# Relative-bias rows of a decoder layer: one row store and one scratch-to-scratch copy in place of four spreads from a four-partition tile

## The chip, the core and the metric

The kernel runs on one core of one Trainium2 chip. The metric is the device time of one execution in microseconds (us). Everything is float32; the large matrix products are made from (high, low) pairs of parts, three matmuls each.

## The reference

One decoder layer on x (1, 512, 2048) with a memory mem (1, 256, 2048):

1. mix: one projection w_in feeds retention (8 heads) and sliding-window attention (16 query heads, 4 key-value heads, window 128) with a sink per head and a relative-position bias; the outputs go through w_o; x <- LN(alpha x + mix).
2. cross-attention with 4 heads of 512 into the 256 memory tokens; x <- LN(alpha x + xa).
3. gated feed-forward (5632 wide) with a causal convolution of width 3 on the gate; x <- LN(alpha x + ff).

What the change touches is the bias of the sliding window:

```
bias   = rel_bias[t5_bucket(max(dist, 0))]        # rel_bias (32 buckets, 16 heads), dist = i + 128 - j
logits = where(valid, q k^T * 64**-0.5 + bias, -inf)
m      = max(max(logits), sink);  p = exp(logits - m)
p      = p / (sum(p) + exp(sink - m))
```

For a head the bias depends on the distance alone, so a row of 255 values per head holds all of it. The 128 x 128 table that the kernel needs has, in partition p, that row from element 127 - p on.

## The kernel before

The layer runs in stages on one core: memory(), swa(), retention(), then the output projection, cross-attention and the feed-forward. Weights come as 1 MB chunks (chunk(), L86, on the SP queue, three raw buffers); ACT makes the high part whi (L73), VectorE the low part wlo (L74), and TensorE runs three matmuls per tile (mm3, L96 to L98).

memory() is the stage around the change. For each of the four cross-attention heads h it makes the keys (4 chunks xa_k) and values (4 chunks xa_v); folds the keys with wq (4 chunks xa_q) into blocks ao, stored to scratch a_sc (L225, SP); then multiplies the values by wo (4 chunks xa_o). This last product is four blocks cb of 24 matmuls of 512 columns each, into PSUM banks of tags B, A, B, A (two banks a tag). A block ends with two copies by VectorE from PSUM to a tile oo (L230), which has two buffers, and two stores o_sc<-oo of 256 KB (L232, SP).

The bias rows are made at the start by swa_tables (L237 to L250): three small loads on ACT's queue, one matmul (L246), and a copy by VectorE to br, a tile of 16 partitions (heads) x 256 (L248). br stays in SBUF. In each head of memory(), after the a_sc stores, swa_spread(h) (L252 to L256) writes four rows of br, each 128 times, to a scratch tensor br_sc of 128 x 4 x 256 (512 KB). The written access pattern is head, copy, element: 4 x 128 x 256. In swa() four tables tb (128 x 4 x 128) are loaded from those tensors on ACT's queue (L286), each partition one element earlier than the one before; VectorE adds them to the logits (L328).

Each engine and each queue works in order. The order of instructions on an engine is chosen by a scheduler that runs the program against a model of its time and may move an instruction ahead of those written before it once its inputs are ready. `keep_in_program_order` (in swa_spread) pins an instruction behind what is written before it on the same engine. Dependencies through scratch tensors are kept by semaphores.

Of the kernel before, what the change touches and what calls it, by code (L numbers as in the profile page):

```python
# [10 lines left out]
F32 = mybir.dt.float32  # L11
# [6 lines left out]
P = 128  # L18
# [6 lines left out]
SH = 16  # L25
# [11 lines left out]
class Layer:  # L37
# [23 lines left out]
        warm = self.cp.tile([P, 1], F32, name="warm")  # L61
        nc.scalar.copy(warm, self.mhalf[:, :1])

# [1 line left out]
    def n(self, s):  # L65
        self.uid += 1
        return f"{s}_{self.uid}"
# [13 lines left out]
        return [self.st.tile([P, 1024], F32R, name=self.n(t), tag=t, bufs=4) for t in ("whi", "wlo")]  # L81

    def chunk(self, src, halves=None):
        """One megabyte of weights, as two halves of (high, low) parts."""
        raw = self.st.tile([P, 2048], F32, name=self.n("raw"), tag="raw", bufs=3)
        self.nc.sync.dma_start(raw, src)  # L86
        res = []
        for h in range(2):
            hi, lo = (halves or self.halves)()
            self.split(hi, lo, raw[:, h * 1024:(h + 1) * 1024])  # L90
            res.append((hi, lo))
        return res
# [11 lines left out]
            self.mm3(ps[:, c], (hi[:, w], lo[:, w]), xs(k, c), k == 0, k == KT - 1)  # L104

    def ws(self, src, xs, n=S, tag="W"):
        """Feature-major product of one 128-column tile: [128 cols, n tokens]."""
        ps = self.bank(tag)
        self.ws_mm(ps, self.chunk(src), xs, slice(0, n))
        return ps  # L110

    def ws_pair(self, srcs, xs, tags=("W", "W")):
        """Two such tiles, the first half of the tokens ahead of the second."""
        pss = [self.bank(t) for t in tags]
        hvs = [self.chunk(s) for s in srcs]
        for c in (slice(0, 256), slice(256, 512)):
            for ps, hv in zip(pss, hvs):
                self.ws_mm(ps, hv, xs, c)
        return pss

    def as_block(self, chunks, xs, w, nt, done, kt=KT, tags="AABB"):
        """Token-major products of one block of w columns, nt token tiles."""
        if w == 512:
            acc = [self.bank(tags[t]) for t in range(nt)]
        else:
            b = [self.bank("A") for _ in range(nt // 2)]
            acc = [b[t // 2][:, t % 2 * 256:t % 2 * 256 + w] for t in range(nt)]
        kk = 1024 // w
        k0 = 0
        for src in chunks:  # L130
            for hi, lo in self.chunk(src):
                for t in range(nt):
                    for q in range(kk):
                        c = slice(q * w, (q + 1) * w)
                        self.mm3(acc[t], xs(k0 + q, slice(t * P, (t + 1) * P)), (hi[:, c], lo[:, c]),
                                 k0 + q == 0 and (w == 512 or t % 2 == 0),
                                 k0 + q == kt - 1 and (w == 512 or t % 2 == 1))
                    if k0 + kk == kt and w == 512:
                        done(t, acc[t])
                    elif k0 + kk == kt and t % 2:  # L140
                        done(t - 1, acc[t - 1])
                        done(t, acc[t])
                k0 += kk

    def as_last(self, hv, xs, w, nt, done, kt=KT):
        """As as_block, token tile by token tile."""
        kk = 1024 // w
        last = None
        for t in range(nt):
            acc = self.bank("AB"[t % 2])  # L150
            with self.tc.issue_after(last.ins) if t else nullcontext():
                for k in range(kt):
                    hi, lo = hv[k // kk]
                    c = slice((k % kk) * w, (k % kk + 1) * w)
                    last = self.mm3(acc[:, :w], xs(k, slice(t * P, (t + 1) * P)), (hi[:, c], lo[:, c]),
                                    k == 0, k == kt - 1)
            done(t, acc[:, :w])
# [4 lines left out]
        self.nc.sync.dma_start(r, src)  # L162
        self.split(self.ah[g], self.al[g], r)

# [1 line left out]
    def memory(self):  # L166
        nc, I = self.nc, self.I
        with ExitStack() as c:
# [38 lines left out]
            for h in range(XH):  # L207
                ks = proj("xa_k", h, pre if h == 0 else None)
                vs = proj("xa_v", h)
                if h == 1:  # L210
                    for g in range(4):
                        r = stage().rearrange("p (k s) -> p k s", k=4)
                        nc.sync.dma_start(r, I["xT"][:, 4 * g:4 * g + 4, :])
                        self.split(self.ah[g], self.al[g], r)
                for fq in range(4):
                    o = mp.tile([P, 4, ML], F32, name=self.n("ao"), tag="ao", bufs=2)
                    for hf, (hi, lo) in enumerate(self.chunk(I["xa_q"][4 * h + fq])):
                        ps = self.bank("T")
                        for i in range(2):
                            for k in range(4):  # L220
                                c = slice((4 * i + k) * P, (4 * i + k + 1) * P)
                                self.mm3(ps[:, i * ML:(i + 1) * ML], (hi[:, c], lo[:, c]), ks(k, slice(0, ML)),
                                         k == 0, k == 3)
                        nc.scalar.copy(o[:, 2 * hf:2 * hf + 2], ps.rearrange("p (i m) -> p i m", i=2))
                    nc.sync.dma_start(self.asc[h // 2][fq][:, :, h % 2 * ML:(h % 2 + 1) * ML], o)  # L225
                self.swa_spread(h)
                for cb in range(4):
                    def done(m, a):
                        o = mp.tile([P, S], F32, name=self.n("oo"), tag="oo", bufs=2)
                        nc.vector.tensor_copy(o, a)  # L230
                        k = 2 * h + m
                        nc.sync.dma_start(self.osc[cb][k // 4][:, k % 4], o)  # L232

                    self.as_block([I["xa_o"][4 * h + cb]], vs, 512, 2, done, 4, "AA" if cb % 2 else "BB")

# [1 line left out]
    def swa_tables(self, mp):  # L237
        nc, I, cp = self.nc, self.I, self.cp
        self.sink = cp.tile([P, SH], F32, name="sink")
        nc.scalar.dma_start(self.sink, I["swa_sinks"].broadcast_to([P, SH]))  # L240
        rb = mp.tile([32, SH], F32, name="rb")
        nc.scalar.dma_start(rb, I["rel_bias"])
        oh = mp.tile([32, 256], F32, name="oh")
        nc.scalar.dma_start(oh, I["c_onehot"])
        ps = self.bank("T")
        nc.tensor.matmul(ps[:SH, :256], rb, oh, start=True, stop=True)  # L246
        br = mp.tile([SH, 256], F32, name="br")
        nc.vector.tensor_copy(br, ps[:SH, :256])  # L248
        self.br = br
        self.brsc = []  # L250

    def swa_spread(self, g):  # L252
        t = self.dr.tile([P, 4, 256], F32, name=f"br_sc{g}")
        src = self.br[4 * g:4 * g + 4].unsqueeze(1).broadcast_to([4, P, 256])
        self.tc.keep_in_program_order(self.nc.sync.dma_start(t.rearrange("p h t -> h p t"), src))
        self.brsc.append(t)  # L256

    def swa(self):
        nc, I, sp = self.nc, self.I, self.sp
# [11 lines left out]
        for g2 in range(2):  # L271
# [9 lines left out]
            tbs = []  # L281
            for gg in range(2):
                tb = sp.tile([P, 4, P], F32, name=self.n("tb"), tag="tb", bufs=2)
                src = self.brsc[2 * g2 + gg]
                ap = bass.AP(tensor=src.tensor, offset=src.offset + 127, ap=[[4 * 256 - 1, P], [256, 4], [1, P]])
                nc.scalar.dma_start(tb, ap)  # L286
                tbs.append(tb)
            qs = {}
# [16 lines left out]
                        self.swa_out(g2, *p, vs)  # L305

    def swa_logits(self, g2, unit, qs, ks, tbs):
        """Probabilities of two heads in one block: column c stands for the one
        token of the window (of this block up to the diagonal, of the previous
        one above it) that lies at c."""  # L310
        nc, sp = self.nc, self.sp
        gg, b, m2 = unit
        lg = sp.tile([P, 2, P], F32, name=self.n("lg"), tag="lg", bufs=3)
# [132 lines left out]
        nc.scalar.activation(o, pt, AF.Copy, scale=gn[:, h:h + 1])  # L446
        return o

# [1 line left out]
    def affine(self, y, pool, gbc, bbc):  # L450
        nc = self.nc
        for q in range(4):
# [7 lines left out]
                nc.gpsimd.tensor_tensor(y[t][:, c], y[t][:, c], B, op=ALU.add)  # L460

    def post(self, y, blocks, xs, kt, lng, own=None):
        """y = norm(alpha * y + x @ w), token-major and in place; y * g + b feature-major."""
        nc, lp = self.nc, self.lp
        bs = [lp.tile([P, 4, 6], F32, name=self.n("lbs"), tag=f"lbs{t}") for t in range(NT)]

# [10 lines left out]
        w = 512  # L477
# [28 lines left out]

        self.as_last(hv, xs, w, NT, fin, kt)

# [1 line left out]
    def scores(self):  # L510
        nc, xp = self.nc, self.lp
        ph = [xp.tile([P, 4, S], F32R, name=f"ph{i}") for i in range(2)]
# [24 lines left out]
                          lambda t, a: soft(hp, t, a))  # L537
        return lambda k, c: (ph[k // 4][:, k % 4, c], pl[k // 4][:, k % 4, c])

# [1 line left out]
    def ffn(self, y):  # L541
        nc, I, fp = self.nc, self.I, self.fp
        cw = self.fp.tile([P, NFF, 4], F32, name="cw")
# [97 lines left out]
                nc.vector.scalar_tensor_tensor(v, v, rs, B[:, c], op0=ALU.mult, op1=ALU.add)  # L641
            nc.sync.dma_start(self.out[0, t * P:(t + 1) * P, c], v)

# [1 line left out]
    def run(self):  # L645
        nc, I = self.nc, self.I
        self.memory()
# [159 lines left out]
```

## Time and profile before

| | us |
|---|---|
| median of 3 runs (2902.71 to 2902.89) | 2902.73 |
| span of the profiled execution, first to last instruction | 2899.5 |
| TensorE busy (matmul) | 2796.2 |
| VectorE busy | 1298.5 |
| ACT (ScalarE) busy | 862.5 |
| POOL busy | 262.8 |

The profile gives the span of one execution; what it leaves out against the median of the runs is 3.2 us around it. PE is TensorE's matmuls and PEld its weight loads, DVE is VectorE, ACT ScalarE, POOL GpSimd; SPq and ACTq are the queues on which SP and ACT issue transfers. An instruction is named by its line, its operation and out<-in. PEclk is the clock granted to TensorE as a share of 2.4 GHz. Matmuls are pipelined, so the busy times of neighbours overlap. A wait is put down to the instruction that ended it.

### The profile page before, as it was taken

The numbers are of one execution on the slowest core, as the hardware profiler recorded it, in microseconds if no ns is written. First come the engines' busy times: TensorE is split into PE (matmuls) and PEld (weight loads), VectorE is DVE, ScalarE is ACT, GpSimd is POOL, SyncE is SP. The second block draws the span as 40 slices with busy tenths as digits, with TensorE's granted clock in tenths as the row PEclk, the third lists the DMA queues.
The fourth block names the chain that finished last, engine by engine and source line by source line (L and its number), as shares of the span: only waits on it lengthen the run. The fifth ranks groups of instructions, "written<-read, shape, count | busy, mean of one in ns | idle before, by whom it ended". The sixth has DMA issues, their size and how long they took to land.

```text
span 2899.5 us, 34839 instructions
## 1 busy us (share of the span) xinstructions
PE 2796.2 (96%) x14642; PEld 2399.3 (83%) x14642; DVE 1298.5 (45%) x1878; ACT 862.5 (30%) x1214; POOL 262.8 (9%) x244
## 2 busy tenths in 40 slices
PE   8789798999999999999999999999999999999997
PEld 8788787889989888978788888888888888888886
DVE  6334333666343443554654333433434343433356
ACT  5333332433222232232432223222222322232331
POOL 0000000223010100160260000000000000000003
PEclk9899898999999999999999999999999999999999
DMA  8656655222322253132232232232222323223241
GB/s 298 193 190 203 199 184 167 80 86 80 102 93 93 81 189 131 59 102 100 76 117 98 91 102 93 96 102 87 102 94 95 102 87 102 93 96 102 89 144 58
DMA packets 72061, 337.64 MB, mean 116 GB/s; under 512 B 7488, under 2 KB 24288, under 8 KB 35552
## 3 DMA queue, kind: packets, MB, share of 16 engines
q1 hardware_dynamic: 65232, 322.99, 32.7%
q10 hardware_dynamic: 6672, 12.43, 1.3%
q8 instruction: 115, 1.88, 0.3%
q14 instruction: 42, 0.34, 0.0%
HBM read 309.17 MB, written 26.21 MB: 116 GB/s over the span
## 4 chain that ended last, share of the span: by engine, by line
PE 61%; DVE 1%; POOL 1%; ACT 1%; issue 0%; DMA 0%; DVEq 0%; ACTq 0%; POOLq 0%
PE psT L96 6%; PE psT L97 6%; PE psT L98 6%; PE psW L96 5%; PE psW L97 5%; PE psW L98 5%; PE psA L96 5%; PE psA L97 5%; PE psA L98 5%; PE psB L96 4%; PE psB L98 4%; PE psB L97 4%; PE psT L495 0%; POOL y L459 0%; ACT xf L503 0%
## 5 line engine op out<-in xcount | busy, mean ns | idle before, releaser
L74 DVE TENSOR_TENSOR wlo<-raw,whi 128x1024 fp32r<-128x1024 f32 x532 | 671.0, 1264 | 1070.2 <-ACT whi L73 1068.4
L73 ACT CAST whi<-raw 128x1024 fp32r<-128x1024 f32 x532 | 557.9, 1051 | 1628.9 <-PE psW L97 597.4
L96 PE MATMUL psW<-ah,whi 128*128 128x512 f32 (+1 forms) x1136 | 443.7, 391 | 0.4 <-ACT ah L73 0.4
L98 PE MATMUL psW<-ah,wlo 128*128 128x512 f32 (+1 forms) x1136 | 442.7, 390 | 0.0
L97 PE MATMUL psW<-al,whi 128*128 128x512 f32 (+1 forms) x1136 | 441.6, 389 | 0.4 <-POOL al L74 0.4
L97 PE MATMUL psT<-al,whi 128*128 128x512 f32 (+1 forms) x720 | 276.8, 384 | 0.0
L98 PE MATMUL psT<-ah,wlo 128*128 128x512 f32 (+1 forms) x720 | 276.7, 384 | 0.0
L96 PE MATMUL psT<-ah,whi 128*128 128x512 f32 (+1 forms) x720 | 276.7, 384 | 0.0
L96 PE MATMUL psA<-whi,ah 128*128 128x256 f32 (+1 forms) x800 | 245.8, 308 | 6.2 <-ACT xp L523 3.0
L97 PEld LDWEIGHTS psW<-al,whi 128*128 128x128 f32 x1136 | 214.8, 189 | 44.0 <-POOL al L74 0.7
L96 PEld LDWEIGHTS psW<-ah,whi 128*128 128x128 f32 x1136 | 214.8, 189 | 43.7 <-ACT ah L73 0.9
L98 PEld LDWEIGHTS psW<-ah,wlo 128*128 128x128 f32 x1136 | 214.9, 189 | 42.4
L97 PE MATMUL psA<-wlo,ah 128*128 128x256 f32 (+1 forms) x800 | 245.1, 306 | 0.0
L98 PE MATMUL psA<-whi,al 128*128 128x256 f32 (+1 forms) x800 | 244.6, 306 | 0.0
L96 PEld LDWEIGHTS psA<-whi,ah 128*128 128x128 f32 x800 | 154.0, 192 | 14.3 <-ACT xp L523 3.5
L97 PEld LDWEIGHTS psA<-wlo,ah 128*128 128x128 f32 x800 | 153.9, 192 | 6.6
L98 PEld LDWEIGHTS psA<-whi,al 128*128 128x128 f32 x800 | 153.9, 192 | 6.5
L98 PEld LDWEIGHTS psT<-ah,wlo 128*128 128x128 f32 x720 | 135.3, 188 | 26.9
L97 PEld LDWEIGHTS psT<-al,whi 128*128 128x128 f32 x720 | 135.3, 188 | 26.9
L96 PEld LDWEIGHTS psT<-ah,whi 128*128 128x128 f32 x720 | 135.3, 188 | 26.8
L98 PE MATMUL psW<-mh,wlo 128*128 128x256 f32 x512 | 145.8, 285 | 1.5 <-DVE wlo L74 1.5
L96 PE MATMUL psW<-mh,whi 128*128 128x256 f32 x512 | 145.9, 285 | 0.9 <-ACT whi L73 0.9
(207 smaller groups left out, 4409.7 us busy)
## 6 DMA issues: line engine op xcount, KB each, us to landing
raw<-in_ffn_up SPq DMA_DIRECT2D x88, 1024.0 KB, 4.8
raw<-in_w_in SPq DMA_DIRECT2D x44, 1024.0 KB, 4.9
raw<-in_ffn_down SPq DMA_DIRECT2D x44, 1024.0 KB, 4.9
raw<-in_xa_v SPq DMA_DIRECT2D x16, 1024.0 KB, 7.0
raw<-in_xa_q SPq DMA_DIRECT2D x16, 1024.0 KB, 4.9
raw<-in_xa_o SPq DMA_DIRECT2D x16, 1024.0 KB, 5.9
raw<-in_w_o SPq DMA_DIRECT2D x16, 1024.0 KB, 4.8
raw<-in_xa_k SPq DMA_DIRECT2D x15, 1024.0 KB, 10.0
```

What stands on the lines that cost most here:

```text
L73: self.nc.scalar.copy(hi, src)
L74: (eng or self.nc.vector).tensor_tensor(lo, src, hi.bitcast(F32), op=ALU.subtract)
L96: mm(ps, a[0], b[0], start=start, stop=False)
L97: mm(ps, a[0], b[1], start=False, stop=False)
L98: return mm(ps, a[1], b[0], start=False, stop=stop)
```

## The change

The rows br are stored once to a scratch tensor brow (16 x 256, 16 KB), on ACT's queue, in swa_tables. swa_spread loses its argument and its pin, and is called in the first head alone: one transfer on ACT's queue reads the 16 KB of brow 128 times (a step of 0 outermost) and writes br_sc, now one tensor of 128 x 4096 (2 MB). The table loads take their rows from it: offset 4 (2 g2 + gg) 256 + 127, and a step of 16 x 256 - 1 = 4095 elements per partition instead of 1023. Comments are removed elsewhere.

```diff
-                self.swa_spread(h)
+                if h == 0:
+                    self.swa_spread()
...
         br = mp.tile([SH, 256], F32, name="br")
         nc.vector.tensor_copy(br, ps[:SH, :256])
-        self.br = br
-        self.brsc = []
-
-    def swa_spread(self, g):
-        t = self.dr.tile([P, 4, 256], F32, name=f"br_sc{g}")
-        src = self.br[4 * g:4 * g + 4].unsqueeze(1).broadcast_to([4, P, 256])
-        self.tc.keep_in_program_order(self.nc.sync.dma_start(t.rearrange("p h t -> h p t"), src))
-        self.brsc.append(t)
+        self.brow = self.dr.tile([SH, 256], F32, name="br_row")
+        nc.scalar.dma_start(self.brow, br)
+
+    def swa_spread(self):
+
+        self.brsc = self.dr.tile([P, SH * 256], F32, name="br_sc")
+        src = bass.AP(tensor=self.brow.tensor, offset=self.brow.offset, ap=[[0, P], [1, SH * 256]])
+        self.nc.scalar.dma_start(self.brsc, src)
...
                 tb = sp.tile([P, 4, P], F32, name=self.n("tb"), tag="tb", bufs=2)
-                src = self.brsc[2 * g2 + gg]
-                ap = bass.AP(tensor=src.tensor, offset=src.offset + 127, ap=[[4 * 256 - 1, P], [256, 4], [1, P]])
+                src = self.brsc
+                ap = bass.AP(tensor=src.tensor, offset=src.offset + 4 * (2 * g2 + gg) * 256 + 127,
+                             ap=[[SH * 256 - 1, P], [256, 4], [1, P]])
                 nc.scalar.dma_start(tb, ap)
```

## Rows read from the trace of the kernel before

**Rows 1.** The page's head and its totals: busy us (share of span) xinstructions.

```profile
span 2899.5 us, 34839 instructions
...
PE 2796.2 (96%) x14642; PEld 2399.3 (83%) x14642; DVE 1298.5 (45%) x1878; ACT 862.5 (30%) x1214; POOL 262.8 (9%) x244
```

**Rows 2.** Waits of TensorE, whole span: us in total, times, longest us.

```profile
PE psA L96 <- DVE oo L230: 66.5, 5, 15.9
```

**Rows 3.** Timeline of VectorE: start us, us, engine line, out<-in, [idle before <-releaser].

```profile
9.17 0.40 DVE L248 COPY br<-psT 16x256 f32<-16x256 f32 x1
...
113.92 0.69 DVE L230 COPY oo<-psA 128x512 f32<-128x512 f32 x1 [21.09 <-DMA o_sc<-oo]
```

**Rows 4.** Timeline of the SP queue in the first head.

```profile
86.00 0.57 SPq L255 DMA_DIRECT2D br_sc<-br  x1
86.69 6.40 SPq L86 DMA_DIRECT2D raw<-in_xa_k  x1
93.13 7.34 SPq L232 DMA_DIRECT2D o_sc<-oo  x2
```

**Rows 5.** Line L232 (o_sc stores): issue ns min/median/max, starts; then landing.

```profile
L232 SPq DMA_DIRECT2D o_sc<-oo x32: 319/320/3687, 93.1 to 457.5; - x32
...
DMA to landing us min/median/max: 2.9/7.5/21.1
```

**Rows 6.** Windows behind a spread: length, busy PE/PEld/DVE/ACT/POOL, PEclk, DMA share, GB/s.

```profile
90.00:92.00 2.00, 2.00 (x11) 1.58 (x10) 0.43 (x2) 1.05 (x1) 0.00 (x0) 1.00 0.22 24
...
104.00:106.00 2.00, 0.00 (x0) 0.00 (x0) 0.00 (x0) 0.00 (x0) 0.00 (x0) 0.50 0.70 127
```

**Rows 7.** Windows of the start, same columns.

```profile
15.00:20.00 5.00, 3.55 (x28) 3.14 (x27) 3.18 (x4) 2.93 (x4) 0.00 (x0) 1.00 1.01 428
20.00:25.00 5.00, 5.00 (x44) 5.00 (x44) 4.11 (x5) 3.30 (x4) 0.00 (x0) 1.00 1.01 421
```

**Rows 8.** Timeline of TensorE: the first and the last of the five waits.

```profile
114.75 0.76 PE L96 MATMUL psA<-whi,kvh 128*128 128x512 f32 x1 [15.87 <-DVE oo L230]
...
454.50 0.36 PE L96 MATMUL psA<-whi,ah 128*128 128x256 f32 x1 [2.87 <-DVE oo L230]
```

**Rows 9.** Windows around the four waits, and of stretches without one, same columns.

```profile
93.12:98.72 5.60, 5.60 (x25) 4.30 (x23) 0.00 (x0) 1.05 (x1) 0.00 (x0) 1.00 0.71 200
...
114.75:123.11 8.36, 8.36 (x25) 6.61 (x26) 4.54 (x5) 1.53 (x2) 0.00 (x0) 0.65 0.82 261
...
224.64:232.70 8.06, 8.06 (x25) 6.36 (x26) 4.54 (x5) 1.52 (x2) 0.00 (x0) 0.68 0.83 258
...
334.23:342.12 7.89, 7.89 (x25) 6.23 (x26) 4.54 (x5) 1.53 (x2) 0.00 (x0) 0.69 0.84 265
...
443.71:454.50 10.79, 7.93 (x24) 6.02 (x25) 6.03 (x8) 2.59 (x3) 0.00 (x0) 0.79 0.81 276
...
454.50:458.57 4.07, 4.07 (x21) 4.07 (x22) 2.82 (x3) 0.00 (x0) 0.00 (x0) 0.58 0.64 183
...
20.00:85.00 65.00, 65.00 (x535) 64.40 (x535) 39.71 (x37) 36.82 (x43) 0.00 (x0) 1.00 0.77 286
```

**Rows 10.** DMA issues: queue, xcount, KB each, median us from issue to landing.

```profile
raw<-in_ffn_up SPq DMA_DIRECT2D x88, 1024.0 KB, 4.8
...
a_sc<-ao SPq DMA_DIRECT2D x16, 512.0 KB, 3.5
...
raw<-in_ln_g ACTq DMA_DIRECT2D x1, 1024.0 KB, 4.7
...
gn<-in_gnT ACTq DMA_DIRECT2D x1, 4.0 KB, 5.0
```

**Rows 11.** Timeline of ACT's queue in the start.

```profile
7.11 0.35 ACTq L372 DMA_DIRECT2D gn<-in_gnT  x1
```

**Rows 12.** Tile tb: its readers and loads, duration ns, first and last start us.

```profile
L328 DVE CUSTOM_DVE_ANT_0 lg<-lg,tb,sink x64: 332/350/456, 520.8 to 699.5; 128x128 f32<-128x128 f32 x64
L286 ACTq DMA_DIRECT2D tb<-br_sc x4: 383/386/1156, 465.2 to 608.3; - x4
```

## The prediction

> **What bounds the kernel now.** I read the totals first: TensorE is busy for 2796.2 of the 2899.5 us span, and no other compute engine passes half [rows 1]. So the time is matmul time plus 103.3 us in which TensorE does nothing, and I asked next who leaves it idle. The waits of TensorE answer: 66.5 us, in only five waits, are the first matmul into a psA bank waiting for a copy to oo (L230) [rows 2]. VectorE's timeline carries it one step back: the copy at 113.92 had waited 21.09 us for an earlier store o_sc<-oo to land, since oo has two buffers [rows 3].
>
> The timeline of the SP queue shows what stands before those stores. In the first head the spread br_sc<-br (L255) is issued at 86.00; the raw load after it takes 6.40 us to issue, and the next two o_sc stores 7.34 together [rows 4], where the median store issue takes 0.32 [rows 5]. While the spread runs the DMA engines are mostly idle: 22% of sixteen busy (3.5 engines), 24 GB/s at 90 to 92 us [rows 6], against 421 to 428 GB/s at 101% when all work [rows 7]. At 24 GB/s the spread's 0.524 MB is 22 us of work. The reading: four engines serve the spread, and a load or store that uses all sixteen lands only when its share on those four is through.
>
> The first stall is 15.87 us long, before the matmul at 114.75; the smallest of the five waits, 2.87 us, stands at 454.50 [rows 8]. The other 66.5 - 2.87 = 63.6 us are four waits of nearly the same length, one per head of memory(), each some 13 us behind that head's spread.
>
> **Part 1, the four spreads go.** The waits: 63.6 us [rows 2, 8]. Then the clock. A block of 24 matmuls of 512 columns takes 5.60 us at full clock (93.12:98.72) [rows 9]. While TensorE idles the granted clock falls to 0.50, the 1.2 GHz level [rows 6], and the same 24 matmuls after the wait take 8.36, 8.06 and 7.89 us in heads 0 to 2: 2.76 + 2.46 + 2.29 = 7.51 us lost [rows 9]. In the last head, from 443.71 to 454.50, the block and the wait of 2.87 us take 10.79, so 10.79 - 5.60 = 5.19 [rows 8, 9]. Behind that wait 21 matmuls of 256 columns take 4.07 us at a mean clock of 0.58 [rows 9]; at the 5.00 us for 44 of the stretch 20:25 they would take 2.39, so 1.68 more [rows 7]. Together 63.6 + 7.51 + 5.19 + 1.68 = **78.0 us**. Between 20 and 85 us, with the same kinds of work and no spread, TensorE is never idle [rows 9], so work that is brought forward meets no other wait that the trace shows.
>
> What is late next where the stall was? The stores' own landing. An oo buffer is used again one block (5.60 us) later. With the copy's 0.69 us [rows 3] and the shortest landing, 2.9 us, its cycle is 3.6 and fits; with the median of 7.5 [rows 5] it is 8.2 and each block after the first would slip by 2.6 us, 7.8 for three, less the one block (5.6) by which a psA bank is freed ahead of its next use: 2.2 us a head, 9 for four. So a new stall of this kind costs 0 to 9 us. I take 0: the median includes the stores of the backlog, and a store twice as large (a_sc, 512 KB) lands in 3.5 us [rows 10].
>
> Four issues on SP disappear too. They cost nothing now, since the loads behind them run ahead into three raw buffers while TensorE works, and give nothing back; without that cover each is below one us.
>
> **Part 2, one row store and one copy are added on ACT's queue.** The 16 KB store brow<-br becomes ready when the copy to br ends, at 9.17 + 0.40 = 9.6 us [rows 3]; the spreading copy waits for it to land. The old spreads were pinned behind what precedes them on SP; the new pair is not. Unpinned ACT transfers float: the gn load (L372), written behind the whole of memory() and swa(), is issued at 7.11 us [rows 11]. So I expect the copy not at 86 us but near 9.6 + 0.4 (issue, as gn's) + 5.0 (landing, as gn's [rows 10]) = 15 us. Queued behind it on ACT are the casts whi, mh and ah of the first loads; VectorE's lo parts wait for those casts, and TensorE for both.
>
> The copy moves 128 x 16 KB = 2.10 MB. No row shows a scratch-to-scratch transfer. Its lower bound is 0, if it runs where the loads have lead. It can't gain: it adds bytes to engines that are already full. As DMA time at 421 GB/s it is 5.0 us [rows 7]. Reading one row many times is no penalty by itself: the ln3 gain, 1 MB fetched from one 8 KB row, lands in 4.7 us where an ordinary MB takes 4.8 [rows 10]. At the removed spreads' rate per engine (24 / 3.5 = 6.9 GB/s, sixteen of them 110) it is 19 us, all of which the start could lose. I take 5 for the whole start, nearest to that broadcast row: from 15 to 20 us the engines are full and TensorE is busy for 3.55 of 5.00 us only [rows 7], so 5.0 us of added traffic delay the raw loads by up to 5.0; some lead hides a part, and ACT standing at the wait for the row's landing adds as much again. Bounds: 0 to 19.
>
> The Trainium skill speaks against such a copy, in "DMA: Bandwidth & Descriptors", section "Bandwidth": it gives about 358 GB/s of HBM bandwidth per core. A copy that reads and writes HBM would carry 4.19 MB across it, 11.7 us by that figure as an estimate, and the sum would be 6.7 us worse. The trace differs for loads, with 421 to 428 GB/s; no row here has a copy within HBM.
>
> **Part 3, the table loads** tb (L286) step 4095 elements from partition to partition instead of 1023, with the same 512-byte runs. The first is issued at 465.2 and first used by VectorE at 520.8 [rows 12]; 55 us cover it, so 0. Uncovered, the slower of two landings would show once per pair of heads, a few us. Removed comments cost nothing.
>
> **Sum.** 78.0 - 5 = 73.0 us gained. The profiled span is 3.2 us below the median of the runs, 2902.73; I carry the difference over to the median: 2902.73 - 73.0 = **2829.7 us**.
>
> **Rivals.**
> *The copy is as slow per engine as the spreads and costs the start (chance 0.07).* For: the cause of that low rate is not in the rows. Against: the broadcast load at full rate. At 19 us: 2902.7 - 78.0 + 19 = 2843.7; with some us of lower clock 2847.
> *The stores themselves hold part of the wait (0.06).* For: the releaser named is a store, and the median landing is long [rows 3, 5]. Against: all five waits on oo stand in the backlog of a spread. If half of the gain stays away: 2902.7 - 39 + 5 = 2869.
> *Nothing moves (0.02).* If the loads and not the spreads held the queue, the same waits return; the 3.5 busy engines speak against it. About 2902.
> *Slower (0.04).* The copy again runs on about four engines. Then 2.10 MB at 24 GB/s take 87 us, in the start, where every 1 MB load needs its share of those four. If all 87 us reach TensorE, with some 3 of lower clock, it is 2902.7 - 78.0 + 90 = 2915. It decides from 78 us of lost start on. For: 3.5 busy engines is what the spreads showed [rows 6]. Against: the copy has 128 rows outermost on both sides where a spread had 4 heads, and it is on another queue than the loads, which are then beside it and not behind it.
> The Trainium skill, same page, section "Why a DMA increments its semaphore by 16 and not by 1", says that the number of engines is the largest up to 16 that divides the outermost size of both sides. That gives 4 for the spread, as the trace has it, and 16 for the copy; by it this rival falls away.
>
> **How the numbers follow.** The forecast has 0.81. Its own range is 2902.7 - 78.0 + 0 = 2825 to 2902.7 - 78.0 + 10 + 9 = 2844. Where the scheduler orders other work anew, some us may go either way, so the low end is 2821; the first rival moves the high end to 2847. What lies above is 0.12 in named rivals, with little below. A measurement of this kernel tells 0.2%, about 6 us, from no change: faster has 0.81 + 0.07 + 0.06 = 0.94, same 0.02, slower 0.04.
>
> **What would show it.** Right: TensorE's wait on oo falls from 66.5 to under 10 us, the raw load after the last a_sc store of a head issues in under 1 us, the clock stays at 1.00 through the four heads, and the last matmul of memory() comes some 70 us earlier. A copy at 10 to 20 us on ACT's queue, with casts waiting about 5 us more for raw loads or for the row, would confirm part 2. Wrong: an o_sc landing above 10 us, TensorE idle for over 10 us anywhere between 20 and 400 us, or a start that ends more than 20 us later.

## The result and the profile after

The changed kernel takes 2828.02 us (median of four runs, 2825.46 to 2831.51) against 2902.72 (four runs): a ratio of 0.9748, 95% interval 0.9734 to 0.9762. That is 74.7 us less; the two profiled spans differ by 2899.5 - 2826.7 = 72.8 us.

The totals of the changed kernel, for [rows 1], and two of its waits of TensorE, for [rows 2] (us in total, times, longest):

```profile
span 2826.7 us, 34831 instructions
...
PE 2787.4 (99%) x14642; PEld 2393.5 (85%) x14642; DVE 1298.1 (46%) x1878; ACT 862.7 (31%) x1214; POOL 263.1 (9%) x244
```

```profile
PE psW L96 <- ACT whi L73: 2.7, 2, 1.4
PE psA L96 <- DVE oo L231: 2.5, 1, 2.5
```

The five waits on oo, 66.5 us, have become one of 2.5. The timeline of the SP queue at the end of the first head shows why: with no spread behind the a_sc store, the raw load is issued in 0.42 us and two o_sc stores in 2.06, for 6.40 and 7.34 in [rows 4].

```profile
90.09 0.52 SPq L225 DMA_DIRECT2D a_sc<-ao  x1
90.87 0.42 SPq L86 DMA_DIRECT2D raw<-in_xa_k  x1
91.70 2.06 SPq L233 DMA_DIRECT2D o_sc<-oo  x2
```

That a_sc store, the last of the first head, stood at 85.43 in the kernel before:

```profile
85.43 0.53 SPq L225 DMA_DIRECT2D a_sc<-ao  x1
```

So the start has become 4.66 us longer. ACT's timeline there has the two new transfers, and the DMA issues say when they landed (KB, median us from issue to landing):

```profile
9.97 0.34 ACTq L251 DMA_DIRECT2D br_row<-br  x1
...
14.93 0.57 ACTq L257 DMA_DIRECT2D br_sc<-br_row  x1
```

```profile
br_sc<-br_row ACTq DMA_DIRECT2D x1, 2048.0 KB, 12.0
...
br_row<-br ACTq DMA_DIRECT2D x1, 16.0 KB, 4.9
```

Windows of the start (columns as in [rows 6]) answer to [rows 7]: TensorE is busy for 2.97 us instead of 3.55 between 15 and 20, and in this execution the granted clock then falls to a mean of 0.67, so that 32 matmuls fit where 44 did. The last row is the stretch behind the remaining wait, at the first product of swa(): 18 matmuls in 3.72 us at 0.54, as behind the same wait before ([rows 9]).

```profile
15.00:20.00 5.00, 2.97 (x22) 2.56 (x22) 2.74 (x4) 2.64 (x4) 0.00 (x0) 0.99 1.06 451
20.00:25.00 5.00, 5.00 (x32) 5.00 (x31) 3.42 (x4) 1.99 (x2) 0.00 (x0) 0.67 0.98 413
...
384.91:388.63 3.72, 3.72 (x18) 3.72 (x19) 1.58 (x2) 0.00 (x0) 0.00 (x0) 0.54 0.81 269
```

Longer windows show where the start lost its time. The first pair is the kernel before, the second the changed kernel, the third another profile of the changed kernel (the run j_after_again below), in which the a_sc store is at 90.69:

```profile
10.00:30.00 20.00, 17.55 (x134) 16.73 (x134) 14.70 (x17) 13.71 (x15) 0.00 (x0) 1.00 1.00 404
30.00:40.00 10.00, 10.00 (x86) 10.00 (x85) 7.80 (x8) 6.98 (x8) 0.00 (x0) 1.00 1.02 421
```

```profile
10.00:30.00 20.00, 17.49 (x118) 16.88 (x118) 10.54 (x13) 9.92 (x12) 0.00 (x0) 0.91 1.00 395
30.00:40.00 10.00, 7.84 (x64) 7.43 (x63) 7.65 (x7) 6.91 (x7) 0.00 (x0) 1.00 1.01 419
```

```profile
10.00:30.00 20.00, 18.13 (x132) 17.49 (x132) 9.54 (x12) 9.11 (x11) 0.00 (x0) 1.00 0.99 379
30.00:40.00 10.00, 6.92 (x44) 6.55 (x43) 9.69 (x9) 7.76 (x9) 0.00 (x0) 0.83 1.01 424
```

Between 30 and 40 us 22 matmuls are missing, because ACT's cast of the first xT piece waits for its load, where it waited 0.43 us before; the casts behind it come late, and TensorE waits for them at 34.06 (the 1.4 above):

```profile
27.09 1.91 ACT L73 CAST ah<-stg 128x2048 fp32r<-128x2048 f32 x1 [4.02 <-DMA stg<-in_xT]
```

At 86 matmuls in 10 us, the 16 that are missing before 30 us and these 22 are 1.9 + 2.6 = 4.5 us, nearly the 4.66; in the second profile they are 0.2 + 4.9 of 5.26. Both are estimates from counts of matmuls.

The account of the 72.8 us: from the first head's last a_sc store to the first product of swa() it was 454.50 - 85.43 = 369.07 us and is 384.91 - 90.09 = 294.82, so 74.25 gained in memory(); 4.66 lost in the start; the remaining 3.2 comes later, between the cross-attention scores and the feed-forward. The second profile of the same kernel has 1.7 there. All eleven profiles with two oo buffers run the same TensorE work from that product on, and need 2441.8 (this one) to 2445.9 us for it (2445.0 before), so this is scatter between executions and not an effect of the change.

### The profile page after: what moved, and what is told of

Same layout as the page of the kernel before. It is cut to its first block, busy times and chain, and to the rows that moved or that the text cites. A ratio compares the mean times of both kernels' runs of the same rounds, so it can differ in the third digit from the quotient of the medians.

```text
span 2826.7 us, 34831 instructions
## 1 busy us (share of the span) xinstructions
PE 2787.4 (99%) x14642; PEld 2393.5 (85%) x14642; DVE 1298.1 (46%) x1878; ACT 862.7 (31%) x1214; POOL 263.1 (9%) x244
## 4 chain that ended last, share of the span: by engine, by line
PE 62%; DVE 1%; POOL 1%; ACT 0%; issue 0%; DMA 0%; DVEq 0%; ACTq 0%; POOLq 0%
PE psT L96 6%; PE psT L98 6%; PE psT L97 6%; PE psW L97 6%; PE psW L98 6%; PE psW L96 6%; PE psA L96 5%; PE psA L98 5%; PE psA L97 5%; PE psB L96 4%; PE psB L97 4%; PE psB L98 4%; POOL y L461 0%; PE psT L497 0%; DVE y L643 0%
```

## The experiments

Three questions were open: whether the four engines explain why the old spreads held the queue; whether it mattered that they were on the loads' queue; and what the longer start is made of.

**Rows stored once, four copies at the old places.**

```diff
+        nc.scalar.dma_start(self.brow, br)
...
-        src = self.br[4 * g:4 * g + 4].unsqueeze(1).broadcast_to([4, P, 256])
-        self.tc.keep_in_program_order(self.nc.sync.dma_start(t.rearrange("p h t -> h p t"), src))
+        src = bass.AP(tensor=self.brow.tensor, offset=self.brow.offset + 4 * g * 256,
+                      ap=[[0, P], [256, 4], [1, 256]])
+        self.tc.keep_in_program_order(self.nc.sync.dma_start(t, src))
```

> Of the change only the form of the spread is kept: the rows are stored once, and in each of the four heads a copy of 512 KB stands where the old spread stood, on SP's queue, pinned, but with 128 rows outermost instead of 4 heads. Same bytes, place and queue. Theory (the spread's four engines hold the queue): the waits of 15.9 us go, TensorE waits on oo under 6 us in all, and the start has no 2 MB copy in it: 2824 us (2820 to 2829). Rival (512 KB at this place hold the stores whatever engines carry them): the four waits stay at 10 us or more each, 2870 to 2903.

Measured: 2828.02 us (2824.48 to 2831.46), ratio 0.974 (0.9724 to 0.9757). Its only wait on oo, which is at the end of memory(), its copies (DMA issues) and its last a_sc store of the first head:

```profile
PE psA L96 <- DVE oo L230: 3.7, 1, 3.7
```

```profile
br_sc<-br_row SPq DMA_DIRECT2D x4, 512.0 KB, 5.8
```

```profile
87.92 0.53 SPq L225 DMA_DIRECT2D a_sc<-ao  x1
```

The theory holds for the waits and the time: the same 512 KB, at the same place in the same queue, hold nothing. So neither one copy instead of four, nor ACT's queue, nor the early place is what gained. But the start was expected back at its old length, and the a_sc store stands at 87.92 without any copy there.

**The old spreads, on ACT's queue.**

```diff
-        self.tc.keep_in_program_order(self.nc.sync.dma_start(t.rearrange("p h t -> h p t"), src))
+        self.tc.keep_in_program_order(self.nc.scalar.dma_start(t.rearrange("p h t -> h p t"), src))
```

> The kernel before with one thing changed: the four spreads, still with 4 heads outermost, are issued on ACT's queue instead of SP's, at the same places. Theory 1 (loads and stores were held because they stood behind the spread in one queue): the waits on oo fall to under 4 us a head, 2823 to 2835 us. Theory 2 (the four engines themselves are taken for 22 us, whichever queue a transfer comes from): at least half of each wait stays, 8 us or more a head, 2855 to 2903 us.

Measured: 2896.27 us, ratio 0.9983 (0.9973 to 0.9992). The first spread is issued at 84.10, a little ahead of the last a_sc store. Theory 2 holds:

```profile
PE psA L96 <- DVE oo L230: 62.8, 5, 15.4
```

The spread shares its queue with no load or store now, and the wait stays. What the old spread takes away is time on DMA engines, not the turn in a queue. In the DMA view of 100 to 102 us both queues (q1 SP's, q10 ACT's; packets, MB, share of 16 engines) crawl:

```profile
q1 hardware_dynamic: 48, 0.11, 28.9%
q10 hardware_dynamic: 41, 0.04, 17.3%
```

**One copy with four outermost.**

```diff
-        src = bass.AP(tensor=self.brow.tensor, offset=self.brow.offset, ap=[[0, P], [1, SH * 256]])
-        self.nc.scalar.dma_start(self.brsc, src)
+        src = bass.AP(tensor=self.brow.tensor, offset=self.brow.offset, ap=[[1024, 4], [0, P], [1, 1024]])
+        self.nc.scalar.dma_start(self.brsc.rearrange("p (g t) -> g p t", g=4), src)
```

> The changed kernel with the copy's 128 x 4096 written as 4 x 128 x 1024, four outermost; same bytes, queue and place in the program. Theory (4 outermost means four engines): it lands after 40 us or more instead of 12.0. If those engines hold back loads of the other queue too, the start costs 20 us or more over the changed kernel: 2848 to 2910. If a transfer beside them, on another queue, takes its turn packet by packet, the start costs at most 10 us more: 2828 to 2838. Rival (the outermost size does not matter): it lands in about 12 us and the time is 2828.

Measured: 2837.19 us (2834.29 to 2838.14), ratio 0.9774 (0.976 to 0.9789), some 9 us over the changed kernel; the a_sc store is at 98.77. Windows, and the DMA view of the first of them:

```profile
45.00:50.00 5.00, 5.00 (x44) 5.00 (x44) 2.92 (x4) 3.48 (x4) 0.00 (x0) 1.00 0.25 104
50.00:55.00 5.00, 5.00 (x44) 5.00 (x43) 2.63 (x2) 1.06 (x2) 0.00 (x0) 1.00 0.26 106
```

```profile
q10 hardware_dynamic: 75, 0.31, 14.9%
q1 hardware_dynamic: 30, 0.21, 10.1%
```

14.9 + 10.1 = 25.0% is four of sixteen engines exactly, shared by the copy and the loads that wait for their part there. So the outermost size sets the engines, as the Trainium skill has it ("DMA: Bandwidth & Descriptors", section "Why a DMA increments its semaphore by 16 and not by 1"). The copy is still running at 55 us, 40 after its issue, and costs what was expected of loads that take turns with it. Yet these four move 104 GB/s together, 26 each, where the old spreads' 3.5 moved 24 together, 6.9 each. So four engines alone were not the old spreads' trouble; but the pieces are larger here, and the source is another.

**Four outermost from the row store, and sixteen outermost from SBUF.** The two factors were taken apart. The first kernel is rows stored once, copied at the old places, but with the old order of four heads:

```diff
+        src = bass.AP(tensor=self.brow.tensor, offset=self.brow.offset + 4 * g * 256,
+                      ap=[[256, 4], [0, P], [1, 256]])
+        self.tc.keep_in_program_order(self.nc.sync.dma_start(t.rearrange("p h t -> h p t"), src))
```

> The four spreads of the kernel before at their place on SP's queue, again with 4 heads outermost and pieces of 1 KB; only the source is changed, from br in SBUF to the row store in scratch. Theory (the low rate per engine comes from reading one SBUF partition over and over; four engines alone would not hold the queue): 4 engines move 1 KB pieces at the rate of ordinary stores, the spread takes 6 to 10 us, the waits of TensorE on oo stay under 3 us a head and the time is 2824 to 2835. Rival (four engines and 1 KB pieces are enough, whatever the source): the waits of 13 us or more a head stay, 2885 to 2903.

The second has no row store; one spread of all 16 rows, straight from br, stands in the first head:

```diff
+        src = self.br.unsqueeze(1).broadcast_to([SH, P, 256])
+        self.tc.keep_in_program_order(
+            self.nc.sync.dma_start(self.brsc.rearrange("p (h t) -> h p t", h=SH), src))
```

> One spread of all 16 rows straight from br, each partition read 128 times, 16 heads outermost, 2 MB, on SP's queue, pinned in the first head; no row store. Theory (each engine reading one SBUF partition moves some 7 GB/s): 16 engines carry 110 GB/s, the spread takes 18 to 20 us and the first head keeps a wait of 8 to 14 us, the three others none: 2832 to 2846. Rival (the low rate comes from using four engines): it takes about 5 us, no wait over 3 us, 2823 to 2829.

Measured: 2837.07 us (2835.52 to 2838.85), ratio 0.9774, and 2845.66 us (2842.70 to 2848.73), ratio 0.9805 (0.9788 to 0.9821). The DMA view while a spread runs nearly alone, first of the kernel before (90 to 92 us), then of four from the row store (90 to 91), then of sixteen from SBUF (94 to 98); columns are packets, MB, share of 16 engines:

```profile
q1 hardware_dynamic: 47, 0.05, 22.3%
```

```profile
q1 hardware_dynamic: 96, 0.09, 27.0%
```

```profile
q1 hardware_dynamic: 370, 0.38, 84.0%
```

Engine time per packet, all about 1 KB: before, 0.223 x 16 x 2 us / 47 = 152 ns; four from the row store, 0.270 x 16 x 1 / 96 = 45 ns; sixteen from SBUF, 0.840 x 16 x 4 / 370 = 145 ns. So on four engines or on sixteen, a piece from br takes over three times as long as a piece from scratch takes on four.

That one partition is read again and again, as the theory for four engines had it, is not the reason. In the run with the old spreads on ACT's queue, the first spread is alone in q10. The DMA view of its first tenth of a microsecond (84.94 to 85.04), in which three pieces follow one another; of a stretch with all four engines at work (85.5 to 86.5); and of its end (109 to 111.3), where the last 7 of 512 pieces come one by one:

```profile
q10 hardware_dynamic: 3, 0.00, 8.5%
```

```profile
q10 hardware_dynamic: 23, 0.02, 20.4%
```

```profile
q10 hardware_dynamic: 7, 0.01, 0.9%
```

That is 0.085 x 16 x 100 ns / 3 = 45 ns a piece at first, 0.204 x 16 x 1000 / 23 = 142 ns in the middle, and 0.009 x 16 x 2300 / 7 = 47 ns at the end, when each of the four rows had been read over a hundred times. A piece that is read alone is as quick as one from scratch (1 KB in 45 ns is 23 GB/s), and four engines together get hardly more than that: 24 GB/s. A store from SBUF is not slow in itself either. The DMA view of an a_sc store in the changed kernel (84 to 85 us), with 1 KB pieces from 128 partitions on all sixteen engines, gives 1.013 x 16 x 1000 / 333 = 49 ns:

```profile
q1 hardware_dynamic: 333, 0.34, 101.3%
```

What is slow is several engines reading br's few partitions at the same time: 24 GB/s from four partitions, 95 from all sixteen. Whether it matters that these partitions are neighbours was not tried.

The 2 MB of the second kernel land after 25.0 us, where 18 to 20 were expected, and the wait appears once, at another place, behind a raw load that landed late:

```profile
br_sc<-br SPq DMA_DIRECT2D x1, 2048.0 KB, 25.0
```

```profile
PE psW L96 <- ACT whi L73: 16.5, 1, 16.5
```

With four engines and the row store the waits on oo are 7.0 us in all, 5.5 of them at the end of memory() and 0.3 to 0.5 in each head:

```profile
PE psA L96 <- DVE oo L230: 7.0, 5, 5.5
```

The time is 2 us above the theory's range for four engines, and the wait with sixteen is 2.5 us longer than the theory's longest. Of the 74 us between the kernel before (2901 to 2902) and copies at the same places with 128 rows outermost (2828), another source gives about 65 (to 2837), and more engines the last 9. Taken the other way round, sixteen engines with the old source give 57 (from 2902.45 to 2845.66, with one spread in place of four), and the source the last 18. Either alone takes most of the waits away, and the shares depend on the order.

**The copy pinned.**

```diff
-        self.nc.scalar.dma_start(self.brsc, src)
+        self.tc.keep_in_program_order(self.nc.scalar.dma_start(self.brsc, src))
```

> The changed kernel with the 2 MB copy pinned behind what is written before it on ACT, so that it is issued near 85 us and not at 14.9. Theory (the copy's bytes in the full start cost 4.7 us): the last a_sc store of the first head is back near 85.4 us and the time falls by 3 to 5 us, to 2823 to 2825. Rival 1 (the wait for the row or the row store itself made the start longer): the start stays at 90 us and the time at 2828. Rival 2 (the copy collides with loads and stores of the first head there): a new wait of 3 us or more in TensorE between 85 and 125 us, 2827 or more.

Measured: 2827.65 us (2827.17 to 2828.31), ratio 0.9743 (0.9729 to 0.9758). Rival 1 holds: the copy, now issued at 87.13, lands in 8.9 us and collides with nothing, but the a_sc store is still late, and the time is the changed kernel's. Of the matmuls 26 are missing before 30 us and 1 between 30 and 40: the copy's part of the loss is gone, and the other part is larger than the changed kernel's 16.

```profile
88.57 0.53 SPq L225 DMA_DIRECT2D a_sc<-ao  x1
```

The waits of SP between 8 and 13 us show a reason that I had not looked for:

```profile
SPq L86 <- DMA lng<-in_ln2T: 2.5, 1, 2.5
```

The first full xa_k load waits for the ln2 table, which it has nothing to do with. It is issued at 11.36 instead of 8.90; in the changed kernel at 10.14. The two programs' instruction lists have the reason. Transfers count their landings on a few semaphores that the scheduler uses in turn, and one more transfer in the start moves this load to the next of them (before, then after):

```
10 L86 DMA raw_13_217<-in_xa_k 128x2048 [waits DMAHW0_49]
10 L86 DMA raw_13_219<-in_xa_k 128x2048 [waits DMAHW1_49]
```

The first was last used by a piece of memT, the second by the ln2 table. In the kernel before it is the second of the two loads that waits for that table.

**The row store alone.** The kernel before, with the store added and nothing reading it:

```diff
+        self.brow = self.dr.tile([SH, 256], F32, name="br_row")
+        nc.scalar.dma_start(self.brow, br)
```

> The kernel before with the row store alone added at the start on ACT's queue; the four spreads stay and nothing reads the stored rows. Theory (the store itself, by shifting which earlier transfer SP's next load waits for, lengthens the start): SP's first full xa_k load is issued at 10.1 us or later instead of 8.9, waiting for the ln2 table, and the last a_sc store of the first head moves from 85.4 to 87 or later, with no copy in the kernel. Rival (only the 2 MB copy lengthens the start): 8.9 and 85.4 stay. The time tells little: 2902.7 or 2 us more.

Measured: 2902.43 us (2899.17 to 2904.02), ratio 1.0001. The wait came as expected, and the delay of the start did not:

```profile
10.07 0.80 SPq L86 DMA_DIRECT2D raw<-in_xa_k  x2
...
85.23 0.53 SPq L225 DMA_DIRECT2D a_sc<-ao  x1
```

So a load that is 1.2 us late can be made up for. In the other kernels with a row store and no copy in the start, the load is issued at 10.23, 10.71 and 11.36 and the a_sc store stands at 86.96, 87.92 and 88.57; there the clock fell to 0.66 or 0.67 between 20 and 25 us, and here it did not. The second profile of the changed kernel agrees: there the load is issued at 10.97, the clock stays at 1.00, and only 2 matmuls are missing at 30 us. That the lower clock is what makes the difference fits these profiles; no run forced it.

**Row store and copy late, then with four oo buffers.** The row store is pinned in the first head and the copy in the second; the second kernel also has `bufs=4` for oo.

```diff
+                if h == 0:
+                    self.brow = self.dr.tile([SH, 256], F32, name="br_row")
+                    self.tc.keep_in_program_order(nc.scalar.dma_start(self.brow, self.br))
+                if h == 1:
+                    self.swa_spread()
...
+        self.tc.keep_in_program_order(self.nc.scalar.dma_start(self.brsc, src))
...
-                        o = mp.tile([P, S], F32, name=self.n("oo"), tag="oo", bufs=2)
+                        o = mp.tile([P, S], F32, name=self.n("oo"), tag="oo", bufs=4)
```

> The changed kernel with the row store pinned in the first head and the copy pinned in the second, so that the start is that of the kernel before. Theory (the row store in the start shifts the counters that SP's next loads wait on, some 2 us, and the copy's bytes cost some 3 more): the last a_sc store of the first head is back at 85.4 (85.0 to 86.0), no new wait over 2 us in the second head, and the time is 4 to 5 us under the changed kernel: 2823.5 (2821 to 2825). Rival (the start varies by itself, and neither matters): a_sc at 87 to 90 and 2826 to 2829.

> As g_late with four oo buffers instead of two. Theory (the last wait on oo, 2.5 us at the end of memory(), and the lower clock behind it come from a store that has not landed): that wait goes, 1.7 us of clock with it, and the time is 3 to 4 us under g_late: 2820 (2817 to 2822). Rival (another wait takes its place there, for the first x or weight parts): within 1 us of g_late.

Measured: 2825.06 us (2823.22 to 2827.56), ratio 0.9733 (0.9719 to 0.9748), for the first kernel, and 2823.22 us (2821.39 to 2823.92), ratio 0.9725 (0.9711 to 0.974), for the second. The first kernel's a_sc store, then the second's wait on oo, and its window from the first product of swa() on:

```profile
85.85 0.53 SPq L225 DMA_DIRECT2D a_sc<-ao  x1
```

```profile
PE psA L96 <- DVE oo L234: 0.3, 1, 0.3
```

```profile
379.84:383.56 3.72, 3.72 (x34) 3.72 (x33) 0.56 (x1) 0.00 (x0) 0.00 (x0) 1.00 0.84 273
```

The start is back. The first kernel's median is 3.0 us under the changed kernel's, short of the 4 to 5 expected, with overlapping intervals. With four buffers the wait is gone and the clock behind it is 1.00: 34 matmuls in 3.72 us, where the changed kernel has 18. But the median is only 1.8 us under that of the first kernel, not 3 to 4, and so between the theory and its rival. The two kernels farthest apart were therefore run again side by side:

> The changed kernel once more, on the same chip as the next run, for a comparison of the two: 2825 to 2830 us.

> The kernel of h_late_oo4 once more, on the same chip as the changed kernel. Theory (start 4 to 5 us shorter, the last wait and its clock some 3 us): 4 to 7 us under the changed kernel. Rival (no difference beyond the scatter of runs): within 2 us of it.

Measured: 2828.82 us (2826.62 to 2830.47) and 2823.65 us (2821.54 to 2827.28), ratios 0.9748 (0.9733 to 0.9762) and 0.9731 (0.9717 to 0.9746). The late version with four buffers is 5.2 us lower here and 4.8 lower in its first comparison (2828.02 against 2823.22). Both agree with the theory's 4 to 7, though the intervals of the ratios still overlap. It is the fastest version found.

## Why the prediction was right, point by point

**The bound and the chain.** Right: the stores' landing held oo, and the spreads held the stores. All four long waits and their clock losses went. With the 2.87 us that stayed in another form left out, the terms give 63.6 + 7.51 + 2.32 = 73.4 us for memory(), and 74.25 were measured.

**The reading of the spread.** "Four engines serve the spread, and a load or store that uses all sixteen lands only when its share on those four is through" is right and not enough. Four engines that read the row store leave 7.0 us of waits. The wait of 16.5 us with sixteen engines on br says less against the reading, since that spread carries four times the bytes. It took both: four engines, and a source that gave those four 24 GB/s together where scratch gave them 94. The rows had the low rate (3.5 engines and 24 GB/s are 6.9 GB/s per engine), and the prediction only used it to price a rival. Also, a queue of its own would not have helped, as the spreads on ACT's queue show; the first argument against the slower rival, 128 rows outermost, holds, and the second, that loads are "beside it and not behind it", is worth little when pieces are slow.

**The wait at the end of memory() and its clock.** Wrong: 2.87 + 1.68 us were to go and 2.5 us of wait and the lower clock stayed. That wait was put down to the backlog of a spread; it comes with two oo buffers, as the kernel with four shows. This is the step that was over by some 4 us (78.0 predicted for part 1, 74.25 measured), and the scatter of 3.2 us in a later stage covered it in the profile.

**The start.** The place of the copy was predicted at 15 us and is 14.93; the row landed in 4.9 us for an assumed 5.0; the start cost 4.66 for an assumed 5. The working behind the 5 is only partly right. The added traffic did delay a load that the casts need, by some 4 us. ACT did not stand at the wait for the row: it was busy with casts when the row landed. And a part came that no step contained, the loss before 30 us. By the counts of matmuls the copy cost 2.6 us in this profile and 4.9 in the second one, and the rest 1.9 and 0.2. The start as a whole is 4.66 and 5.3 us longer in these two; -0.2 to 3.1 in kernels with the row store and no copy there, which lose nothing between 30 and 40 us; and -0.2 to 0.4 in kernels with neither. That the row store's part comes by the wait for another transfer's counter is likely but not shown: the load is late in every kernel that has the store in the start, and time is lost before 30 us only where the clock also fell. So the 5 is near the mark in part by luck.

**The copy's rate.** Nothing scratch-to-scratch was in the trace of before, and the nearest row, the broadcast load, was the right one: where the engines were not full, the 2 MB landed in 8.9 us. By the 358 GB/s of the Trainium skill ("DMA: Bandwidth & Descriptors", section "Bandwidth"), a core's share when its neighbour streams too, 11.7 us would be needed for reading and writing, as an estimate. Here 4.19 MB in 8.9 us are 471 GB/s, so that figure does not bound this copy.

**The sum.** 73.0 us predicted, 72.8 by spans and 74.7 by medians. The 3.75 us that part 1 had too much and the 3.2 us of scatter in a later stage cancel, so the closeness is luck; the size of the four waits and of their clock losses is not.

## What to carry to other kernels

When a transfer with little in it holds up others, divide its rate by the engines that are busy: a low rate per engine points at its source or its pieces, a low number of engines at its outermost size. The two have different remedies, and here either remedy alone took most of the waits away. Rows that must be repeated many times are better stored once to scratch and copied from there than spread by several engines at once from a tile of a few partitions, and a queue of its own does not make the latter harmless. Before moving a small transfer into a crowded start, look at what the loads behind it will wait for: one transfer more can make a load wait for a landing that has nothing to do with it.

## What the runs showed that was not expected

A 1 KB piece from a tile of 16 partitions took a DMA engine 45 to 47 ns when it was read alone, and 142 to 152 ns with four or sixteen engines at the tile at once; from scratch it took 45 ns with four engines at once. The order of waits in the start changed with one added 16 KB store: the first full load waited 1.3 to 2.5 us for a table loaded on another queue, and the start of the kernels without an early copy was then 0 to 3 us longer, by one profile of each.
